# Where the high part of a split f32 weight chunk is rounded: by a cast on ScalarE, or by a transfer from GpSimd's queue

## The chip, the cores and the metric

The kernel runs on one core of a Trainium2 chip, in one launch. The metric is device time in microseconds (us), the median of repeated runs. Before the change it is 1033.94 us, the median of 3 runs that lie between 1033.83 and 1033.95.

## The reference

One decoder layer on 512 tokens of width 1024, in float32. What matters here is the long row of matrix products, each with weights of its own:

```python
h = rmsnorm(x, norm_mix_g)                        # x: 512 x 1024
proj = h @ w_in                                   # 10 sections of 512 columns, 3 x 1024 gate columns
cb, cc, ch, sq, sk, sv, rq, rk, rv, rg, gate_logits = split(proj)
branches = stack([short_conv_mixer(cb, cc, ch),   # 512 wide each
                  stick_breaking_attention(sq, sk, sv),      # 8 heads x 64
                  retention(rq, rk, rv, rg)])                # 4 heads x 128
up = einsum('bsnw,nwd->bsnd', branches, w_branch)
x = x + sum(sigmoid(gate_logits + b_gate) * up) @ w_o
h = rmsnorm(x, norm_xa_g)                         # cross-attention into 256 memory tokens, 4 heads
x = x + memory_attention(h, rmsnorm(mem), w_xq, w_xkv, w_xo)
h = rmsnorm(x, norm_mlp_g)
x = x + square(relu(h @ w_up)) @ w_down           # hidden width 4096
out = rmsnorm(x, final_g)
```

## The kernel before, in words

**Products in parts.** TensorE multiplies operands of the type fp32r, which is shorter than f32. So the kernel splits every f32 operand into a high part (the value rounded to fp32r) and a low part (what is left), and makes a product of three matmuls: high by high, high by low, low by high. This is `mm3`, lines 234 to 236. The residual stream has four token tiles of 128 rows (`x`, 128 x 1024). Each is normalised (`norm_begin`, `norm_end`: two squares with sums on ScalarE, L354; a mean on VectorE, L358; a power on GpSimd, L348, called `rstd`; a scaling on VectorE, L376, called `xn`), transposed by TensorE in eight 128 x 128 pieces (L385, into the PSUM banks called `at`), and split into `hT_h` and `hT_l` (a ScalarE cast on L223, a VectorE subtraction on L224).

**Weights as a stream.** All weights lie in DRAM as chunks of 128 x 1024 f32 (512 KB). One `Stream` holds them in the order in which the program uses them. For a chunk, SyncE's queue loads it into one of three buffers called `w_raw`; then `parts_of` takes buffers of a pool called `w_part`, 11 in number (`WBUFS`), and writes the high part (ScalarE cast, L111) and the low part (VectorE subtraction, L112). There are two kinds of chunk:

- `Plain`, 144 chunks: used as they are. One chunk feeds 24 matmuls of 512 columns, or more of fewer columns.
- `Seven`, 18 entries of two chunks: a product of a 2 x 2 block matrix made with seven block products in place of eight (L290, 256 columns each). Its weights are first combined on VectorE into `w_mix`, and then split by `parts_of` too.

**What sets the order.** The program is a list of items, `plan`; each names its chunks, and before an item runs, `pump` makes the parts of its chunks and of two more steps (`AHEAD`). The Tile framework then orders the instructions of each engine itself, from a timeline of its own, and adds the semaphores. Each engine works in its order, and a DMA queue (of SyncE, ScalarE, GpSimd) in the order in which its engine issues. When an instruction changes its engine or its cost, the order of others may change too.

**The start.** The first item issues loads of `x` tile 0, the gain `g`, two weight chunks, tile 1, a weight chunk, tiles 2 and 3. The first product is the v projection of the stick-breaking attention (`items_m` with `tok_outer`): four weight chunks, all four used for token tile 0, then for tile 1, and so on, with the normalisation of the next tile between. The accumulators of the four tiles are `mm_177`, `mm_234`, `mm_291` and `mm_348`; their normalised tiles are `xn_111`, `xn_202`, `xn_259` and `xn_316`, and the transposes of these `at_121` and `at_130`, `at_216` and `at_225`, `at_273` and `at_282`, `at_330` and `at_339`. A finished accumulator is split into `sb_v`. The four weight chunks' high parts are `w_part_143`, `w_part_149`, `w_part_155` and `w_part_161`, the low parts `w_part_144`, `w_part_150`, `w_part_156` and `w_part_162`.

**Gates and MLP.** In the later gates (`gates7`) a `Seven` entry for the gate is followed by a `Plain` chunk of `w_branch` (`w_br`). In each of the four MLP rounds `Seven` entries of `w_up` are followed by eight `Plain` chunks of `w_down`.

Of the kernel before, what the change touches and what calls it, by code (L numbers as in the profile page):

```python
# [10 lines left out]
F32 = mybir.dt.float32  # L11
F32R = mybir.dt.float32r
AF = mybir.ActivationFunctionType
ALU = mybir.AluOpType

P = 128
# [11 lines left out]
CW = 1024  # L28
# [5 lines left out]
RAWS, WBUFS, AHEAD = 3, 11, 2  # L34
# [4 lines left out]
def trunk_kernel(ctx: ExitStack, tc: tile.TileContext, x, mem, par, rot, dqd, kdec, g_mix, g_xa, g_mem, g_mlp,  # L39
                 g_fin, w_in, w_gate, w_br, w_o, w_xq, w_xk, w_xv, w_xo, w_up, w_up7, w_down, out):  # L40
    nc = tc.nc
    te, act, dve, pool = nc.tensor, nc.scalar, nc.vector, nc.gpsimd

    const = ctx.enter_context(tc.tile_pool(name="const", bufs=1))
    wpool = ctx.enter_context(tc.tile_pool(name="wpool", bufs=1))
# [18 lines left out]
    class Split:  # L64


        def __init__(self, name, n, cols=512):
            self.per = 1024 // cols
            self.n, self.cols = n, cols
            self.h = [unit(name + "_h", (P, self.per, cols)) for _ in range(n // self.per)]  # L70
            self.l = [unit(name + "_l", (P, self.per, cols)) for _ in range(n // self.per)]
# [31 lines left out]
    def parts_of(src):  # L103
        n = src.shape[1]
        part = lambda: wpool.tile([P, CW], F32R, name="w_part", bufs=WBUFS)
        if 2 * n <= CW:
            both = part()
            wh, wl = both[:, :n], both[:, n:2 * n]
        else:
            wh, wl = part(), part()  # L110
        act.copy(out=wh, in_=src)  # L111
        dve.tensor_tensor(out=wl, in0=src, in1=wh.bitcast(F32), op=ALU.subtract)  # L112
        return wh, wl

    class Plain:


        def __init__(self, t, c):
            self.loads = [(t, c)]
            self.steps = [lambda raw: parts_of(raw[0])]  # L120
            self.parts = []

        def get(self):
            return self.parts[0]
# [1026 lines left out]
```

## Time and profile before

| | |
|---|---|
| median of 3 runs | 1033.94 us (1033.83 to 1033.95) |
| the profiled execution | 1033.71 us, of which 1032.0 us are the span of the profile |
| TensorE, matmuls | busy 1015.5 us, 98% of the span, 5636 matmuls |
| VectorE | 648.8 us, 63% |
| ScalarE | 500.7 us, 49% |
| GpSimd | 66.2 us, 6% |
| read from HBM | 103.31 MB, 102 GB/s over the span with what is written |
| chain of work that ended last | TensorE 97%, DMA 1% |

A row of the timeline has the start in us, the duration, the engine (PE is TensorE, DVE is VectorE, ACT is ScalarE, POOL is GpSimd, SPq is SyncE's DMA queue), the line, the operation, the program's names for the operands, the shape and, in brackets, how long the engine was idle before and what ended that. Matmuls overlap: one starts before the last has ended, so the distance between two starts, the step, tells their rate. In the rows of groups stand the count, the busy time, the mean of one in ns, and the idle time before them with what ended most of it. In the table of windows, each engine has its busy time in the stretch with the number of instructions, in the order PE, PEld (weight loads), DVE, ACT, POOL; then come TensorE's granted clock (1.00 is full speed), the share of the DMA engines' time, and GB/s. In the list of waits stand the total, the number and the longest. In the lists of transfers, the last number is the median time from issue to landing.

### The profile page before, as it was taken

What the parts mean: (1) busy time and instruction counts of PE and PEld (TensorE: products, weight loads), DVE (VectorE), ACT (ScalarE), POOL (GpSimd) and SP (SyncE); (2) the same over time, 40 slices, a digit from 0 to 9 for tenths busy, and PEclk for the clock granted to TensorE, in tenths of its full rate; (3) what the DMA queues carried; (4) which work ended last, traced back from release to release, by engine and by line L of the source; (5) the groups of instructions that cost most, each with busy time, mean ns of one, the idle gap of its engine ahead of it and who ended that gap; (6) DMA issues with size and microseconds to landing.
All of it is one profiled execution on the core that took longest, in us unless ns stands there. A gap on an engine that the chain in (4) does not pass through costs nothing.

```text
span 1032.0 us, 14325 instructions
## 1 busy us (share of the span) xinstructions
PE 1015.5 (98%) x5636; PEld 884.9 (86%) x5636; DVE 648.8 (63%) x992; ACT 500.7 (49%) x887; POOL 66.2 (6%) x118
## 2 busy tenths in 40 slices
PE   6999999999999999999999999999999999999997
PEld 4888888888888889998898888898889989989985
DVE  5567777856563796784584555466947566565643
ACT  6465567766532154463463444345416624643741
POOL 1101112321110000000100000000000000000000
PEclk9999999999999999999999999999999999999999
DMA  6322233213122212335354213223222321332222
GB/s 265 103 102 81 83 104 102 82 42 123 62 87 79 100 62 83 103 119 198 133 184 163 82 47 118 81 83 123 86 79 82 125 92 71 124 123 80 103 85 81
DMA packets 29876, 106.33 MB, mean 103 GB/s; under 512 B 3569, under 2 KB 3569, under 8 KB 29809
## 3 DMA queue, kind: packets, MB, share of 16 engines
q1 hardware_dynamic: 27216, 98.05, 27.7%
q10 hardware_dynamic: 2592, 7.37, 2.0%
q8 instruction: 44, 0.72, 0.3%
q14 instruction: 24, 0.19, 0.1%
HBM read 103.31 MB, written 2.10 MB: 102 GB/s over the span
## 4 chain that ended last, share of the span: by engine, by line
PE 97%; DMA 1%; DVE 0%; ACT 0%; SPq 0%; issue 0%; DVEq 0%; POOLq 0%; POOL 0%
PE mm L235 24%; PE mm L234 24%; PE mm L236 24%; PE p L290 17%; PE at L385 1%; PE o L546 1%; PE aT L512 1%; DMA w_raw<-in_w_in_dram 1%; PE z L488 1%; PE z L489 0%; PE xsc L236 0%; PE xsc L235 0%; PE xsc L234 0%; PE ro L693 0%; PE sc L667 0%; PE xpp L929 0%
## 5 line engine op out<-in xcount | busy, mean ns | idle before, releaser
L112 DVE TENSOR_TENSOR w_part<-w_raw,w_part 128x1024 fp32r<-128x1024 f32 (+1 forms) x180 | 210.9, 1176 | 168.1 <-PE mm L235 75.2
L111 ACT CAST w_part<-w_raw 128x1024 fp32r<-128x1024 f32 (+1 forms) x180 | 180.6, 1006 | 135.2 <-PE mm L236 79.1
L234 PE MATMUL mm<-hT_h,w_part 128*128 128x512 f32 (+1 forms) x512 | 193.6, 379 | 0.0
L235 PE MATMUL mm<-hT_l,w_part 128*128 128x512 f32 (+1 forms) x512 | 193.3, 378 | 0.0
L236 PE MATMUL mm<-hT_h,w_part 128*128 128x512 f32 (+1 forms) x512 | 193.0, 378 | 0.0
L290 PE MATMUL p<-mix_h,w_part 128*128 128x256 f32 x576 | 112.2, 283 | 0.5 <-ACT sv_s L297 0.5
L236 PEld LDWEIGHTS mm<-hT_h,w_part 128*128 128x128 f32 x512 | 96.4, 188 | 17.1
L234 PEld LDWEIGHTS mm<-hT_h,w_part 128*128 128x128 f32 x512 | 96.2, 188 | 16.8
L235 PEld LDWEIGHTS mm<-hT_l,w_part 128*128 128x128 f32 x512 | 96.5, 188 | 16.4
L235 PE MATMUL mm<-w_part,u_h 128*128 128x512 f32 x256 | 99.8, 390 | 0.0
L234 PE MATMUL mm<-w_part,u_h 128*128 128x512 f32 x256 | 98.6, 390 | 0.0
L236 PE MATMUL mm<-w_part,u_l 128*128 128x512 f32 x256 | 98.2, 389 | 0.0
L290 PEld LDWEIGHTS p<-mix_h,w_part 128*128 128x128 f32 x576 | 93.4, 192 | 1.4 <-ACT sv_s L297 0.7
L290 PE MATMUL p<-hT_h,w_part 128*128 128x256 f32 x432 | 84.4, 283 | 0.0
L290 PE MATMUL p<-mix_l,w_part 128*128 128x256 f32 x288 | 81.5, 283 | 0.0
L290 PEld LDWEIGHTS p<-hT_h,w_part 128*128 128x128 f32 x432 | 70.1, 192 | 0.8
L111 ACT CAST w_part<-w_mix 128x1024 fp32r<-128x1024 f32 x36 | 37.8, 1051 | 55.9 <-PE mm L235 37.5
L112 DVE TENSOR_TENSOR w_part<-w_mix,w_part 128x1024 fp32r<-128x1024 f32 x36 | 44.0, 1221 | 26.7 <-ACT w_part L111 20.0
L290 PE MATMUL p<-hT_l,w_part 128*128 128x256 f32 x216 | 60.7, 283 | 0.0
L236 PEld LDWEIGHTS mm<-w_part,u_l 128*128 128x128 f32 x256 | 48.1, 188 | 9.8
L235 PEld LDWEIGHTS mm<-w_part,u_h 128*128 128x128 f32 x256 | 48.1, 188 | 9.5
L234 PEld LDWEIGHTS mm<-w_part,u_h 128*128 128x128 f32 x256 | 47.9, 188 | 9.5
(211 smaller groups left out, 1813.2 us busy)
## 6 DMA issues: line engine op xcount, KB each, us to landing
w_raw<-in_w_in_dram SPq DMA_DIRECT2D x52, 512.0 KB, 3.4
w_raw<-in_w_up_dram SPq DMA_DIRECT2D x32, 512.0 KB, 3.6
w_raw<-in_w_down_dram SPq DMA_DIRECT2D x32, 512.0 KB, 3.4
w_raw<-in_w_br_dram SPq DMA_DIRECT2D x12, 512.0 KB, 3.4
w_raw<-in_w_gate_dram SPq DMA_DIRECT2D x12, 512.0 KB, 3.5
w_raw<-in_w_o_dram SPq DMA_DIRECT2D x8, 512.0 KB, 3.5
w_raw<-in_w_xk_dram SPq DMA_DIRECT2D x8, 512.0 KB, 4.2
w_raw<-in_w_xv_dram SPq DMA_DIRECT2D x8, 512.0 KB, 3.5
```

The lines of the kernel that those rows point to most:

```text
L111: act.copy(out=wh, in_=src)
L112: dve.tensor_tensor(out=wl, in0=src, in1=wh.bitcast(F32), op=ALU.subtract)
L234: te.matmul(ps, lh, rh, start=first, stop=False)
L235: te.matmul(ps, lh, rl, start=False, stop=False)
L236: te.matmul(ps, ll, rh, start=False, stop=last)
L290: te.matmul(ps[:, :256], x[:, k, :], y, start=first and k == 0 and i == 0, stop=k == 3 and i == 2, skip_group_check=True)
L385: te.transpose(ps[:, k * P:(k + 1) * P], xn[:, c * P:(c + 1) * P], ident)
L488: te.matmul(z[:, :s], q[:, e, tsl], S["skh", hp][:, e, :s], start=True, stop=False)
L512: te.transpose(aps[:, sb * P:(sb + 1) * P], a[:, sb * P:(sb + 1) * P], ident)
L546: te.matmul(dst, vv, rhs, start=sb == 0 and i == 0, stop=sb == nblk and i == 1, skip_group_check=True)
```

## The change

A `Plain` chunk no longer goes through `parts_of`. Its high part is made by a second transfer of the same chunk from DRAM, issued from GpSimd's queue, from f32 to a tile of the type fp32r, so that the transfer rounds. SyncE still loads the chunk into `w_raw`, because VectorE's subtraction needs the f32 values. `Seven` entries keep ScalarE's cast.

```diff
         def __init__(self, t, c):
             self.loads = [(t, c)]
-            self.steps = [lambda raw: parts_of(raw[0])]
+            self.steps = [self.step]
             self.parts = []
+
+        def step(self, raw):
+            t, c = self.loads[0]
+            wh, wl = [wpool.tile([P, CW], F32R, name="w_part", bufs=WBUFS) for _ in range(2)]
+            pool.dma_start(out=wh, in_=t[c])
+            dve.tensor_tensor(out=wl, in0=raw[0], in1=wh.bitcast(F32), op=ALU.subtract)
+            return wh, wl
```

Seven lines are added, so lines behind them count 7 more: L234 to L236 become L241 to L243, L385 becomes L392, L354 becomes L361, L223 becomes L230; the new transfer is L126 and the new subtraction L127. ScalarE has 711 instructions in its order where it had 855, 144 fewer; GpSimd has 144 transfers more.

**TensorE at the start.** Before, the transposes of the second token tile (`at_216`, `at_225`) stand behind 19 matmuls of the first tile; the rows around them:

```order
L236 MATMUL mm_177<-w_part_155,hT_l_109 128x512
L234 MATMUL mm_177<-w_part_161,hT_h_106 128x512 [waits Activation_49]
L385 MATMUL at_216<-ident_73,xn_202 128x128 [waits DVE_49]
L385 MATMUL at_216<-ident_73,xn_202 128x128 x3
L385 MATMUL at_225<-ident_73,xn_202 128x128 x4
L235 MATMUL mm_177<-w_part_162,hT_h_106 128x512 [waits DVE_49]
L236 MATMUL mm_177<-w_part_161,hT_l_110 128x512
```

After, they stand behind the first six, and from there the matmuls of the first two tiles take turns; where a transferred chunk is used first, TensorE waits for GpSimd's queue (DMASW):

```order
L241 MATMUL mm_177<-w_part_143,hT_h_103 128x512
L242 MATMUL mm_177<-w_part_144,hT_h_103 128x512
L243 MATMUL mm_177<-w_part_143,hT_l_107 128x512
L392 MATMUL at_216<-ident_73,xn_202 128x128 [waits DVE_49,Activation_49]
L392 MATMUL at_216<-ident_73,xn_202 128x128 x3
L392 MATMUL at_225<-ident_73,xn_202 128x128 [waits Activation_49]
L392 MATMUL at_225<-ident_73,xn_202 128x128 x3
L241 MATMUL mm_177<-w_part_149,hT_h_104 128x512 [waits DMASW1_49]
L241 MATMUL mm_234<-w_part_143,hT_h_103 128x512 [waits Activation_49]
```

The last matmul of `mm_177` has moved next to the last ones of `mm_234`, five rows ahead of the third tile's transposes:

```order
L243 MATMUL mm_177<-w_part_161,hT_l_110 128x512
L242 MATMUL mm_234<-w_part_162,hT_h_106 128x512
L243 MATMUL mm_234<-w_part_161,hT_l_110 128x512
L241 MATMUL mm_234<-w_part_161,hT_h_106 128x512
L242 MATMUL mm_234<-w_part_162,hT_h_106 128x512
L243 MATMUL mm_234<-w_part_161,hT_l_110 128x512
L392 MATMUL at_273<-ident_73,xn_259 128x128 [waits DVE_49,PE_49,Activation_49]
```

So 48 matmuls of two tiles now end together, and the third tile's transposes stand right behind them.

**ScalarE at the start.** Before, from the first copy of a finished accumulator (`sb_v`) on:

```order
L223 CAST sb_v_139<-mm_177 128x4x64 [waits PE_49]
L223 CAST hT_h_104<-at_216 128x2x128 [waits DVE_49]
L223 CAST hT_h_106<-at_225 128x2x128 [waits DVE_49]
L223 CAST sb_v_141<-mm_177 128x4x64 [waits DVE_49]
L354 ACTIVATE xn_259,ss_260<-x_86 128x512 [waits DMAHW0_49]
L354 ACTIVATE xn_259,ss_260<-x_86 128x512
L354 ACTIVATE xn_316,ss_317<-x_87 128x512 [waits DMAHW1_49]
L354 ACTIVATE xn_316,ss_317<-x_87 128x512
L223 CAST sb_v_139<-mm_234 128x4x64 [waits PE_49]
```

After, from the same copy on:

```order
L230 CAST sb_v_139<-mm_177 128x4x64 [waits PE_49]
L230 CAST sb_v_141<-mm_177 128x4x64 [waits DVE_49]
L361 ACTIVATE xn_259,ss_260<-x_86 128x512 [waits DMAHW0_49]
L361 ACTIVATE xn_259,ss_260<-x_86 128x512
L230 CAST sb_v_139<-mm_234 128x4x64 [waits PE_49]
L361 ACTIVATE xn_316,ss_317<-x_87 128x512 [waits DMAHW1_49]
L361 ACTIVATE xn_316,ss_317<-x_87 128x512
L230 CAST sb_v_141<-mm_234 128x4x64 [waits DVE_49]
```

The squares of the third tile (`xn_259`) still stand behind the copies of `mm_177`, whose last matmul has moved; those of the fourth (`xn_316`) stand behind a copy of `mm_234` now.

**GpSimd at the start.** After, its transfers and the powers of the norms share one order; before it had the powers alone:

```order
L126 DMA w_part_143<-in_w_in_dram 128x1024
masks.py:199 ISA
masks.py:199 AFFINE_SELECT ident_73<-ident_73 128x128 [waits Pool_49]
L355 TENSOR_TENSOR rstd_118<-ms_116,half_78 128x1 [waits DVE_49,Pool_49]
L126 DMA w_part_149<-in_w_in_dram 128x1024
L355 TENSOR_TENSOR rstd_209<-ms_207,half_78 128x1 [waits DVE_49]
L126 DMA w_part_155<-in_w_in_dram 128x1024
L126 DMA w_part_161<-in_w_in_dram 128x1024
L126 DMA w_part_167<-in_w_in_dram 128x1024
L126 DMA w_part_173<-in_w_in_dram 128x1024
```

The third and later chunks' transfers stand behind the second tile's power (`rstd_209`).

**In the gates.** Before, ScalarE's cast of a `w_br` chunk stands at the place where its buffer comes free (w_part_3386 and w_part_3392 belong to the next `Seven` entry):

```order
L111 CAST w_part_3380<-w_raw_3269 128x1024 [waits DMAHW5_49,PE_49]
L744 ACTIVATE gt_3348<-mm_3323,prm_82 128x512 [waits PE_49,Activation_49]
L223 CAST mix_h_3117<-mix_3258 128x512 [waits DVE_49]
L111 CAST w_part_3386<-w_raw_3376 128x512 [waits DMAHW6_49,PE_49]
L111 CAST w_part_3392<-w_mix_3389 128x1024 [waits DVE_49,PE_49]
```

After, these are GpSimd's rows there; each transfer waits for TensorE's last use of its buffer:

```order
L355 TENSOR_TENSOR rstd_3086<-r_ve_3084,half_78 128x4 [waits DVE_49]
L126 DMA w_part_3380<-in_w_br_dram 128x1024 [waits DMASW1_49,DMASW2_49,DVE_49,PE_49]
L126 DMA w_part_3544<-in_w_br_dram 128x1024 [waits DMASW2_49,DMASW3_49,DVE_49,PE_49]
L126 DMA w_part_3708<-in_w_br_dram 128x1024 [waits DMASW3_49,DMASW4_49,DVE_49,PE_49]
L126 DMA w_part_3878<-in_w_br_dram 128x1024 [waits DMASW4_49,DMASW5_49,DVE_49,PE_49]
L126 DMA w_part_4048<-in_w_br_dram 128x1024 [waits DMASW5_49,DMASW6_49,DVE_49,PE_49]
L126 DMA w_part_4218<-in_w_br_dram 128x1024 [waits DMASW6_49,DMASW7_49,DVE_49,PE_49]
```

The step "buffer free, cast, subtraction" has become "buffer free, transfer, subtraction". On VectorE the subtraction now waits for that transfer, with work for the next entry behind it:

```order
L736 TENSOR_TENSOR gt_3348<-mm_3350,gt_3348 128x512 [waits PE_49]
L127 TENSOR_TENSOR w_part_3381<-w_raw_3269,w_part_3380 128x1024 [waits DMAHW5_49,DMASW2_49]
L144 TENSOR_TENSOR w_mix_3529<-w_raw_3378,w_mix_3529 128x512 [waits DVE_49]
L112 TENSOR_TENSOR w_part_3386<-w_raw_3376,w_part_3386 128x512 [waits Activation_49]
L737 TENSOR_TENSOR mg_2718<-mg_2718,gt_3348 128x512 [waits DVE_49]
```

Ten transferred chunks stand close to the buffer's release. Counted in TensorE's order after the change, between the matmul that frees the buffer and the first that reads the new content:

| high part | weights | matmuls between |
|---|---|---|
| `w_part_3380` | `w_br` | 14 of 512 columns, 36 of 256 |
| `w_part_3544` | `w_br` | 2 of 512, 58 of 256 |
| `w_part_3708` | `w_br` | 2 of 512, 60 of 256 |
| `w_part_3878` | `w_br` | 2 of 512, 47 of 256 |
| `w_part_4048` | `w_br` | 2 of 512, 58 of 256 |
| `w_part_4218` | `w_br` | 2 of 512, 68 of 256 |
| `w_part_4809` | `w_xk` | 19 of 512, 16 of 128, 2 of 256 |
| `w_part_7346`, `w_part_8146`, `w_part_8946` | `w_down` | 49 of 256, each |

## The prediction, made before the changed kernel ran

> **What bounds the kernel now.** I read the page's busy shares and chain first, then the span in three stretches, then who TensorE waits for, then the groups that the change touches, the transfers, and last the first 30 us in order of time.
>
> ```profile
> span 1032.0 us, 14325 instructions
> PE 1015.5 (98%) x5636; PEld 884.9 (86%) x5636; DVE 648.8 (63%) x992; ACT 500.7 (49%) x887; POOL 66.2 (6%) x118
> PE 97%; DMA 1%; DVE 0%; ACT 0%; SPq 0%; issue 0%; DVEq 0%; POOLq 0%; POOL 0%
> ...
> 0.00:30.00 30.00, 20.74 (x87) 15.91 (x88) 17.98 (x34) 18.34 (x42) 5.50 (x16) 1.00 0.60 228
> 30.00:1025.00 995.00, 994.51 (x5550) 868.97 (x5549) 628.54 (x955) 481.66 (x844) 60.18 (x101) 1.00 0.29 99
> 1025.00:1032.00 7.00, 0.21 (x1) 0.00 (x0) 2.26 (x4) 0.72 (x2) 0.55 (x1) 0.85 0.23 84
> ...
> PE at L385 <- DVE xn L376: 9.0, 2, 8.5
> PE p L290 <- ACT sv_s L297: 0.5, 1, 0.5
> ```
>
> The chain is TensorE for 97%. From 30 to 1025 us it is idle for 995.00 - 994.51 = 0.49 us, all of it in its one wait for ScalarE. So what ScalarE does there costs nothing, and there is nothing to win there. TensorE's only real idle time is 9.3 us in the first 30, and the tail. A loss, however, shows in full wherever a weight comes later than TensorE wants it.
>
> ```profile
> L112 DVE TENSOR_TENSOR w_part<-w_raw,w_part 128x1024 fp32r<-128x1024 f32 (+1 forms) x180 | 210.9, 1176 | 168.1 <-PE mm L235 75.2
> L111 ACT CAST w_part<-w_raw 128x1024 fp32r<-128x1024 f32 (+1 forms) x180 | 180.6, 1006 | 135.2 <-PE mm L236 79.1
> q1 hardware_dynamic: 27216, 98.05, 27.7%
> w_raw<-in_w_br_dram SPq DMA_DIRECT2D x12, 512.0 KB, 3.4
> w_raw<-in_w_down_dram SPq DMA_DIRECT2D x32, 512.0 KB, 3.4
> x<-in_x_dram SPq DMA_DIRECT2D x4, 512.0 KB, 8.0
> ```
>
> **The change, part by part.** Removed: 144 of the 180 casts, 144 x 1.006 = 145 us of ScalarE. Worth 0 in the 995 us stretch, whose cover is TensorE itself. The subtraction keeps its count and its 1.18 us; SyncE's loads stay. Added: 144 transfers of 512 KB, 75.5 MB. SyncE's queue used 0.277 x 1032 = 286 us of the sixteen engines for 98.05 MB, or 187 chunks: 1.53 us a chunk. Another 144 make 220 us, a share of 0.21 on top of 0.29. If the rounding transfer moves as fast as the plain one, there is room, so 0; bound above under the rivals. GpSimd's queue takes the 144 issues between its own masks and powers; in the attention part, counted in rows of TensorE's order times the steps below, the masked tile is read 8 us or more after its scores, and an issue of about 1 us (two of its 0.55 us operations, below) twice in that chain fits. A transfer there waits for a buffer that was freed long before its own use, so that a mask queued behind it on GpSimd rarely waits with it. 0, and at most a few tenths a mask if that is wrong.
>
> What costs is order and latency, at two kinds of places.
>
> **The first 30 us.** These are the rows the terms come from; in before, the second token tile's normalisation ran while TensorE worked off the first tile.
>
> ```profile
> 2.73 0.64 SPq L396 DMA_DIRECT2D x<-in_x_dram  x1
> 7.04 1.29 DVE L376 SCALAR_TENSOR_TENSOR xn<-x,rstd,g_bc 128x1024 f32<-128x1024 f32 x1 [0.74 <-POOL rstd L348]
> 8.47 1.94 PE L385 MATMUL at<-ident,xn 128*128 128x128 f32 x8 [8.47 <-DVE xn L376]
> 10.53 0.79 PE L234 MATMUL mm<-w_part,hT_h 128*128 128x512 f32 x1
> 15.01 0.63 ACT L354 ACTIVATE xn<-x 128x512 f32<-128x512 f32 x1
> 15.45 0.63 PE L235 MATMUL mm<-w_part,hT_h 128*128 128x512 f32 x1
> 15.88 0.55 PE L236 MATMUL mm<-w_part,hT_l 128*128 128x512 f32 x1
> 16.26 0.39 PE L234 MATMUL mm<-w_part,hT_h 128*128 128x512 f32 x1
> 16.49 0.40 PE L235 MATMUL mm<-w_part,hT_h 128*128 128x512 f32 x1
> 18.55 1.10 PE L385 MATMUL at<-ident,xn 128*128 128x128 f32 x8 [0.51 <-DVE xn L376]
> 21.14 0.37 ACT L223 CAST sb_v<-mm 128x256 fp32r<-128x256 f32 x1 [1.09 <-PE mm L236]
> 21.55 0.43 DVE L224 TENSOR_TENSOR sb_v<-mm,sb_v 128x256 fp32r<-128x256 f32 x1
> 22.01 0.37 ACT L223 CAST sb_v<-mm 128x256 fp32r<-128x256 f32 x1
> 22.28 0.64 ACT L354 ACTIVATE xn<-x 128x512 f32<-128x512 f32 x1
> 23.52 0.62 ACT L354 ACTIVATE xn<-x 128x512 f32<-128x512 f32 x1
> 23.65 0.16 DVE L358 SCALAR_TENSOR_TENSOR ms<-ss 128x1 f32<-128x1 f32 x1 [0.46 <-ACT xn L354]
> 23.89 0.55 POOL L348 TENSOR_TENSOR rstd<-ms,half 128x1 f32<-128x1 f32 x1 [6.72 <-DVE ms L358]
> 24.47 1.28 DVE L376 SCALAR_TENSOR_TENSOR xn<-x,rstd,g_bc 128x1024 f32<-128x1024 f32 x1
> 26.39 1.03 PE L385 MATMUL at<-ident,xn 128*128 128x128 f32 x8
> 28.02 1.04 PE L385 MATMUL at<-ident,xn 128*128 128x128 f32 x8
> ```
>
> Term 1, when the first two token tiles (48 matmuls) are done. Before, the third tile's transposes follow them at 26.39. In the changed order only 6 matmuls stand ahead of the second tile's transposes, and 42 behind. Their input starts with ScalarE's squares of the second x tile, at 15.01 before. With no casts ahead of them I put these at 13, between 12.2 (2.73, where SyncE issues that load, plus the 8.0 of its row, plus one chunk more in front) and 15.0. From the squares to the end of the normalised tile takes 24.47 + 1.28 - 22.28 = 3.47, so transposes start at 16.5. Warm, they take 1.10 and 42 matmuls at 0.227 (steps as from 16.26 to 16.49) 9.5: done at 27.1, +0.7. Slow, as the first ones are (steps of 0.43 until 16.26, 5.7 us after the first matmul), the transposes take 1.94 and half of another 5.7 us is lost: 30.8, +4.4. Which of them depends on whether 3 us of work with 2 us of idleness behind it counts towards full speed; no row says, and I take the middle, **+2.6**. GpSimd's queue has a wait in this stretch that SyncE's has not: four of the first six transfers stand behind the second tile's rstd, at 13 + 24.44 - 22.28 = 15.2. Issued there, the first lands 5 us later, at 20.2 (the price below); TensorE wants it 17 of the 42 matmuls in, at 17.6 + 3.9 = 21.5. Covered by 1.3; at 8.0 it would be 1.7 late.
>
> Term 2, the third tile. ScalarE now has its squares behind both copies of the first tile's v (mm_177), and that bank is only complete 5 matmuls before the 48 end. From that copy to the normalised tile the rows above run from 21.14 to 24.47 + 1.28 = 25.75: 4.6 us, and 0.1 to the transpose. The copy starts 0.44 after the last matmul on mm_177 starts; TensorE has 6 steps, 1.36 us, from that start. 0.44 + 4.7 - 1.36 = **3.8 us idle**, against none at 26.39 before. The fourth tile's squares follow the next copy (0.37) on ScalarE, its VectorE part follows a subtraction (0.4): its transposes start about 2.7 after the third's, where 28.02 - 26.39 = 1.6 of work is there: **1.0 us idle**. Sum 4.8, fixed by the order and hardly by any transfer.
>
> The trace shows speed falling after idleness once: the last stretch has a clock of 0.85 over 7 us, so half speed for 2.1 us, beginning 4.9 us after the last matmul. The Trainium skill ("TensorE: Matmul & The Clock Gate", Part 1) has half rate after an idle window of about 3.4 us and full rate after a busy one. By that rule a stall of 3.8 us may cost another 1.7 us (half of 3.4) behind it, and the sum would be 9.9 and not 8.2; the trace agrees in kind, at 4.9 us, and does not show 3.8.
>
> **Ten tight buffers.** Rows of TensorE's order between the last matmul on a buffer's old content and the first on its new one, times the steps, give 13 to 40 us in steady stretches. In ten places, listed with the change, they give 5.9 to 8.6 us, at 0.227 for 512 columns and 0.12 for 256, as here:
>
> ```profile
> 773.97 23.17 PE p L290 x193
> ```
>
> A cast fills such a buffer in 1.0 us. The transfer's time from the freeing matmul is not in the trace: at least SyncE's 3.4, at most the 8.0 of the crowded start. Nearest are the 3.4 rows, same size and place; GpSimd's issue (its small operations take 0.55) and the two signals make it 5 to 6. At 5 nothing is late. At 6, three down chunks miss by 0.1 each, and three first quarters of a gate's next weights, whose subtraction stands behind the transferred chunk's on VectorE, by about 0.4: 1.5 in all. I take half, **+0.8**. The Trainium skill ("DMA: Bandwidth & Descriptors", Anatomy of one DMA) gives such a transfer 2.0 us and its bytes at 436 GB/s, an estimate of 3.2 us without the issue; by it the term would be 0 and the sum 7.4.
>
> **Sum.** 2.6 + 4.8 + 0.8 = 8.2 us on the profiled execution, 1033.71 (span 1032.0 and 1.7 around it): 1041.9. The median of the runs is 0.2 above that execution: **1042**.
>
> **Rivals.** (a) Transfers are late: at 8 us the ten places miss by 0.5, 0.6, 0.35, 1.9, 0.6, 0, 1.7 and three times 2.1, in sum 12, the quarters add 1 or 2, and the first transfer behind the rstd 1.7: 1034 + 7.4 + 15 = 1056. For it: the 8.0 row and SyncE's load of the same chunk beside it. Against: in these places the queues hold one or two chunks. 0.18. (b) The rounding transfer is slower a byte, and DMA becomes the bound. A plain chunk feeds 24 x 0.227 = 5.45 us of matmuls; 1.53 of it goes to the raw load, so this decides from 3.9 us a chunk, 2.6 times the plain one. At 3 times, 0.68 us on 144 chunks: 98 us, 1130. Nothing here speaks for it. 0.06. (c) Not slower: ScalarE's relief brings the second tile's squares forward by 2 us (15.01 to 13) and term 2 vanishes, because the third tile's load or copies fall earlier than I read. 1034 - 2 = 1032, faster; it decides only if TensorE waits less than 2 us in the rows of the order, where I count 4.8. 0.07. (d) The change not doing what it says: ScalarE has exactly 144 instructions fewer in the order, so the casts are gone; if the transfer did not round, the time would be the same.
>
> **Chances.** Mine, 1037 to 1046: 0.60. The same with the start half hidden, 1036 to 1037: 0.09. (a), 1046 to 1059: 0.18. (b), above: 0.06. (c): 0.07, of which 0.04 within 0.2% (2 us, about what a measurement of this kernel tells from no change) and 0.03 faster. So slower 0.93. The range 1037 to 1059 leaves out about 0.12 below ((c) and half of the half-hidden start) and 0.06 above.
>
> **What would show it.** Right: ScalarE's busy time near 355 us, DMA share near 0.5; in the first 35 us a TensorE wait for xn of 3 to 4 us and one near 1; TensorE idle under 2 us in all from there to the tail. Wrong: no such wait (term 2), full matmul speed by 17 us (term 1 near 0.7), or TensorE waits for w_part or a DMA in the gate and down stages of more than 3 us (a), or spread over the whole span (b).

## The result, and the profile after

The changed kernel takes 1044.37 us (median of 3 runs, 1043.09 to 1045.06) against 1033.94: slower by 10.4 us. The ratio is 1.0099, 95% interval 1.0076 to 1.0122. The forecast was 1042, between 1037 and 1059. The profiled execution takes 1043.09 us, 9.4 more than that of before, where the sum had 8.2.

The page of the changed kernel, the lines that answer to those of before: span, busy time of the engines, the queues (q1 is SyncE's, q0 GpSimd's), and the chain.

```profile
span 1041.4 us, 14473 instructions
PE 1017.2 (98%) x5636; PEld 886.1 (85%) x5636; DVE 650.5 (62%) x992; ACT 362.7 (35%) x743; POOL 142.9 (14%) x262
q1 hardware_dynamic: 27216, 98.05, 26.6%
q0 software_dynamic: 20736, 75.51, 22.6%
PE 97%; DMA 1%; ACT 1%; DVE 0%; issue 0%; SPq 0%; POOL 0%; DVEq 0%; POOLq 0%
```

ScalarE has lost 138 us of work (500.7 to 362.7), and the time has grown: TensorE is the chain as before. GpSimd's 144 transfers took 0.226 x 1041.4 = 235 us of the sixteen DMA engines, 1.63 us a chunk; SyncE's plain loads 0.266 x 1041.4 = 277 us for 187, 1.48 us a chunk. So a rounding transfer costs a tenth more than a plain one, and the engines are half busy.

Where the 9.4 us went shows in one matmul, the first of the attention scores on its line (L488 before, L495 after). The two rows are from the timelines of before and of after:

```profile
55.21 0.22 PE L488 MATMUL z<-sb_kh,sb_q 128*128 128x128 f32 x1
62.69 0.22 PE L495 MATMUL z<-sb_kh,sb_q 128*128 128x128 f32 x1
```

It starts 7.48 us later; so 7.5 of the 9.4 us are lost ahead of it, and 1.9 in the 970 us that follow. The start, in the changed kernel's timeline (start, duration, and in brackets the idle time before the row and what ended it):

```profile
12.89 0.63 ACT L361 ACTIVATE xn<-x 128x512 f32<-128x512 f32 x1
15.11 1.28 DVE L383 SCALAR_TENSOR_TENSOR xn<-x,rstd,g_bc 128x1024 f32<-128x1024 f32 x1 [0.69 <-POOL rstd L355]
16.54 1.94 PE L392 MATMUL at<-ident,xn 128*128 128x128 f32 x8 [3.47 <-DVE xn L383]
28.13 0.39 PE L243 MATMUL mm<-w_part,hT_l 128*128 128x512 f32 x1
28.29 0.37 ACT L230 CAST sb_v<-mm 128x256 fp32r<-128x256 f32 x1 [0.49 <-DVE sb_v L231]
28.56 0.63 ACT L361 ACTIVATE xn<-x 128x512 f32<-128x512 f32 x1
32.19 1.21 PE L392 MATMUL at<-ident,xn 128*128 128x128 f32 x8 [3.67 <-DVE ss L375]
34.60 1.73 PE L392 MATMUL at<-ident,xn 128*128 128x128 f32 x7
```

The second tile's squares run at 12.89 and its transposes at 16.54, where TensorE has waited 3.47 us. The 48 matmuls of two tiles end with the step from 28.13, at 28.36; before, that point was 26.39, so 2.0 us are lost. Then the third tile's squares, behind the copy at 28.29, start at 28.56, and its transposes at 32.19, 3.8 us after the matmuls. The fourth tile's follow 2.41 us later, 0.8 more than before (28.02 - 26.39 = 1.63). That makes 6.6 us; the last 0.9 are lost behind it, and the clock says how. In the windows below (busy time of PE, PEld, DVE, ACT, POOL, then the granted clock), each row is one window of the grid on which the clock changes:

```profile
12.50:15.91 3.41, 0.57 (x3) 0.13 (x1) 1.54 (x4) 1.65 (x5) 1.40 (x3) 1.00 1.03 413
15.91:19.33 3.42, 2.79 (x11) 2.62 (x12) 2.45 (x5) 1.02 (x3) 1.29 (x3) 0.50 1.11 420
19.33:22.74 3.41, 3.41 (x17) 2.76 (x16) 3.04 (x5) 0.37 (x1) 0.00 (x0) 1.00 1.11 405
29.57:32.98 3.41, 0.79 (x7) 0.82 (x8) 2.33 (x6) 2.19 (x9) 0.95 (x2) 1.00 0.00 0
32.98:36.39 3.41, 3.31 (x14) 2.36 (x13) 2.96 (x6) 1.70 (x5) 0.15 (x1) 0.50 0.02 5
```

The stretches of constant clock last 3.41 us or a multiple of it. A window of this grid in which TensorE was busy only 0.57 or 0.79 us is followed by one at half speed. So each of the two waits costs twice: once itself, and once in the window behind it. Behind the third tile's wait, the slow matmuls also fill the time in which TensorE would otherwise have waited for the fourth tile, so that the list of waits below has no row for it.

Behind the start the only waits of TensorE are for a copy on ScalarE, L304 after and L297 before, now three times where it was one. From the list of TensorE's waits of after, the timeline at the second of the three, and the copy that answers to it in before:

```profile
PE at L392 <- DVE xn L383: 11.7, 2, 8.2
PE at L392 <- DVE ss L375: 3.7, 1, 3.7
PE p L297 <- ACT sv_s L304: 1.5, 3, 0.5
PE mm L242 <- DVE w_part L127: 0.3, 1, 0.3
...
890.65 0.63 ACT L1017 ACTIVATE relu<-sv 128x512 f32<-128x512 f32 x1
891.18 0.35 ACT L304 COPY sv_s<-p 128x256 f32<-128x256 f32 x1
891.59 0.39 PE L297 MATMUL p<-mix_h,w_part 128*128 128x256 f32 x1 [0.49 <-ACT sv_s L304]
879.75 0.36 ACT L297 COPY sv_s<-p 128x256 f32<-128x256 f32 x1
```

ScalarE does a relu of 512 columns ahead of the copy for which TensorE waits. In before the same copy ran at 879.75, 2.85 us ahead of the same matmul (882.60), and nothing waited. That is order again, in two MLP rounds. The 0.49 us of idle time understate what such a wait costs: the matmuls there start 0.12 us apart, and this one starts 0.77 us behind the one before it (890.82). TensorE's lag behind the kernel before is 7.86 us at the first matmul on w_down (736.81 against 728.95) and 9.31 at its last matmul (1034.13 against 1024.82), so the two added waits cost about 0.7 us each, 1.4 in all. The other 0.5 of the 1.9 us are in steps too small to name. No wait for a transferred chunk stands in the list behind the start; the row for w_part is the first chunk's, at 10.93.

### The profile page after: what moved, and what is told of

It reads as the page before. It is cut to its first block, busy times and chain, and to the rows that moved or that the text cites. A ratio compares the mean times of both kernels' runs of the same rounds, so it can differ in the third digit from the quotient of the medians.

```text
span 1041.4 us, 14473 instructions
## 1 busy us (share of the span) xinstructions
PE 1017.2 (98%) x5636; PEld 886.1 (85%) x5636; DVE 650.5 (62%) x992; ACT 362.7 (35%) x743; POOL 142.9 (14%) x262
## 4 chain that ended last, share of the span: by engine, by line
PE 97%; DMA 1%; ACT 1%; DVE 0%; issue 0%; SPq 0%; POOL 0%; DVEq 0%; POOLq 0%
PE mm L241 24%; PE mm L242 24%; PE mm L243 24%; PE p L297 17%; PE at L392 1%; PE o L553 1%; DMA x<-in_x_dram 1%; PE aT L519 1%; PE z L495 1%; PE z L496 0%; PE xsc L243 0%; PE xsc L242 0%; PE xsc L241 0%; PE ro L700 0%; PE sc L674 0%; PE xpp L936 0%
## 5 line engine op out<-in xcount | busy, mean ns | idle before, releaser
L127 DVE TENSOR_TENSOR w_part<-w_raw,w_part 128x1024 fp32r<-128x1024 f32 x144 | 176.9, 1230 | 121.2 <-PE mm L242 47.2
L241 PE MATMUL mm<-hT_h,w_part 128*128 128x512 f32 (+1 forms) x512 | 194.2, 380 | 0.0
L243 PE MATMUL mm<-hT_h,w_part 128*128 128x512 f32 (+1 forms) x512 | 193.2, 377 | 0.0
L297 PE MATMUL p<-mix_h,w_part 128*128 128x256 f32 x576 | 112.0, 283 | 1.5 <-ACT sv_s L304 1.5
L243 PEld LDWEIGHTS mm<-hT_h,w_part 128*128 128x128 f32 x512 | 96.4, 188 | 17.4
L241 PEld LDWEIGHTS mm<-hT_h,w_part 128*128 128x128 f32 x512 | 96.5, 188 | 16.5
L243 PE MATMUL mm<-w_part,u_l 128*128 128x512 f32 x256 | 99.7, 390 | 0.0
L241 PE MATMUL mm<-w_part,u_h 128*128 128x512 f32 x256 | 98.7, 389 | 0.0
L297 PEld LDWEIGHTS p<-mix_h,w_part 128*128 128x128 f32 x576 | 93.1, 191 | 2.8 <-ACT sv_s L304 2.1
L297 PE MATMUL p<-hT_h,w_part 128*128 128x256 f32 x432 | 83.7, 283 | 0.0
L297 PE MATMUL p<-mix_l,w_part 128*128 128x256 f32 x288 | 81.2, 283 | 0.0
L297 PEld LDWEIGHTS p<-hT_h,w_part 128*128 128x128 f32 x432 | 70.0, 192 | 1.0
L297 PE MATMUL p<-hT_l,w_part 128*128 128x256 f32 x216 | 60.9, 283 | 0.0
L243 PEld LDWEIGHTS mm<-w_part,u_l 128*128 128x128 f32 x256 | 48.1, 188 | 9.6
L241 PEld LDWEIGHTS mm<-w_part,u_h 128*128 128x128 f32 x256 | 47.9, 188 | 9.8
L297 PEld LDWEIGHTS p<-mix_l,w_part 128*128 128x128 f32 x288 | 55.1, 191 | 0.7
```

Source lines behind the costliest of these rows:

```text
L127: dve.tensor_tensor(out=wl, in0=raw[0], in1=wh.bitcast(F32), op=ALU.subtract)
L241: te.matmul(ps, lh, rh, start=first, stop=False)
L243: te.matmul(ps, ll, rh, start=False, stop=last)
L297: te.matmul(ps[:, :256], x[:, k, :], y, start=first and k == 0 and i == 0, stop=k == 3 and i == 2, skip_group_check=True)
```

## The experiments

All ran against the kernel before, which took 1033.7 to 1033.8 us each time.

**The first six chunks cast, the rest by transfer.**

```diff
-            self.steps = [self.step]
+            self.steps = [self.step if Plain.n >= 6 else lambda raw: parts_of(raw[0])]
+            Plain.n += 1
```

> The first six plain chunks keep ScalarE's cast, the other 138 come by transfer. ScalarE's order at the start is that of the kernel before again. Theory (the loss lies in the order of the first 47 us, 7.4 us of it in the trace, and 1.9 us more in small waits for ScalarE's copies in the MLP rounds and steps elsewhere): 1035 to 1037 us, no wait for xn over 0.5 us beside the very first, the waits of 0.5 us for sv_s still there. Rival (the 75 MB of added transfers make weights late, or tight buffers do): nearly all of the loss stays, 1042 to 1044.

Measured: 1038.32 us (1036.70 to 1040.27), ratio 1.0042 (1.0029 to 1.0055). The start is that of before to 0.1 us: the attention's first score matmul starts at 55.33. Its waits behind the start, and the timeline at the wait for x_p:

```profile
PE p L300 <- ACT sv_s L307: 1.5, 3, 0.5
PE xpp L939 <- DVE x_p L931: 0.6, 1, 0.6
...
630.55 1.23 DVE L130 TENSOR_TENSOR w_part<-w_raw,w_part 128x1024 fp32r<-128x1024 f32 x1 [2.08 <-DMA w_part<-in_w_xo_dram]
632.19 0.52 PE L939 MATMUL xpp<-ident,x_p 128*128 128x128 f32 x3 [0.60 <-DVE x_p L931]
```

So the start's loss is gone with the casts, as expected, but 4.5 us are left where 1 to 3 were expected, and its runs spread over 3.6 us, where those of before stay within 0.4. Its profiled run is one of the quicker ones (1036.98) and shows only 2.8 us in its span. The theory was incomplete. Of these 2.8 us, 1.4 are the two added waits in the MLP rounds as above, and 1.0 is lost at 632 us, where TensorE's lag grows from 0.3 to 1.3. There a transferred chunk is late: VectorE stands 2.08 us until a chunk of w_xo, issued 6.0 us earlier (624.53), has landed, and `x_p`, for which TensorE waits, stands behind that subtraction. The transfers of w_xo next to it landed in 3.7 to 4.6 us. So a late transfer can cost TensorE time without a wait for w_part in TensorE's list.

**Only the first four chunks by transfer.**

```diff
+            self.steps = [self.step if Plain.n < 4 else lambda raw: parts_of(raw[0])]
+            Plain.n += 1
```

> The opposite: only the first four plain chunks come by transfer, 140 keep the cast. Theory (order of the start): 1041 to 1043 us, with the wait of 3.7 us for the third tile's xn and two half-speed stretches of 3.4 us, as in the changed kernel, and shift of 7.4 us against the kernel before at 60 us. Rival (bytes and late weights over the whole span): 1034 to 1035.

Measured: 1042.59 us (1041.13 to 1044.44), ratio 1.0083 (1.0069 to 1.0098). Four transfers of 144, 2 of 75 MB, make 8.8 us. The rival is out: not bytes, but the order that these four casts held up. The same score matmul starts at 64.79, 9.6 us late, 2.1 more than in the changed kernel. The windows on its clock grid say why:

```profile
12.03:15.44 3.41, 0.75 (x3) 0.27 (x2) 1.63 (x5) 1.60 (x5) 1.26 (x3) 1.00 1.05 412
15.44:18.86 3.42, 2.65 (x11) 2.48 (x12) 2.45 (x4) 1.02 (x3) 0.37 (x1) 0.50 1.09 420
18.86:22.27 3.41, 3.41 (x10) 2.64 (x9) 3.19 (x5) 0.57 (x2) 0.00 (x0) 0.50 0.76 268
...
32.51:35.92 3.41, 2.58 (x10) 2.27 (x11) 2.75 (x7) 1.03 (x4) 2.03 (x4) 0.50 0.00 0
35.92:39.34 3.42, 3.42 (x13) 3.03 (x12) 2.48 (x8) 2.10 (x6) 0.59 (x2) 0.50 0.02 5
```

The grid lies 0.47 us earlier here than in the changed kernel, 2.65 and 2.58 us of work fall into the half-speed windows in place of 2.79 and 3.31, and half speed lasts two windows each time. The same order thus costs 1 to 2 us more or less by where the grid happens to lie. Whether this is also why the runs of kernels with these waits spread over 2 to 3 us is not shown: the slowest run here, 1044.44, has a mean granted clock of 0.996, and the profiled one, 1043.54, has 0.992, so the slower one spent less time at half speed.

**The normalisations ahead of the v projection, all 144 transfers kept.**

```diff
+    for t in range(1, NT):
+        item(lambda t=t: norm_x0(t))
     for t in range(NT):
         plan.append(sv[2 * t])
-        if t < NT - 1:
-            item(lambda t=t: norm_x0(t + 1))
         plan.append(sv[2 * t + 1])
```

> All 144 transfers stay; the normalisations of tiles 2 to 4 are written ahead of the v projection, so that ScalarE's squares no longer stand behind the copies of the first accumulator. Theory (second term: squares behind copies, 3.8 and 1.0 us of idle time and a half-speed stretch behind them, about 5 us in all): 1038 to 1040.5 us, without the wait of 3.7 us. Rival (the third tile's wait is one for its load, delayed by the transfers): the wait only changes its name, 1043 to 1045.

Measured: 1040.20 us (1038.89 to 1042.31), ratio 1.0065 (1.0052 to 1.0078), as the theory had it. The wait of 3.7 us is gone, and the score matmul starts at 58.56, 4.1 us ahead of the changed kernel's. The third tile did not wait for its load, but for ScalarE's squares behind the copies.

**Idle matmuls in the wait.**

```diff
+    def spin(n, of):
+        ps, w = atps("spin"), of()
+        for _ in range(n):
+            te.matmul(ps[:, :P], w, w, start=True, stop=True)
...
+        if t == 1:
+            item(lambda: spin(30, lambda: S["v"][2][:, 0, 0, :]))
```

> The changed kernel with 30 idle matmuls of 128 columns, whose result nobody reads, behind the first 48 matmuls: they run in the 3.8 us in which TensorE waits for the third tile. Nothing else in the order moves. Theory (the idle time itself costs a half-speed stretch of 3.4 us behind it, worth 1 to 1.7 us): the stretch from 33.0 to 36.4 us has full speed, and the time is 0.9 to 1.7 us below the changed kernel's. Rival (the clock falls for another reason, or what it costs is hidden by the fourth tile's wait): the same time within 0.3 us, or more by what the matmuls overrun.

Measured: 1043.23 us (4 runs, 1042.26 to 1044.13), 1.1 below the changed kernel, but the runs of the two overlap, so the time alone doesn't decide. The clock does:

```profile
15.40:18.80 3.40, 2.55 (x10) 2.44 (x11) 2.43 (x4) 0.95 (x3) 1.50 (x3) 0.50 1.09 422
18.80:22.25 3.45, 3.45 (x9) 2.65 (x8) 3.28 (x5) 0.44 (x2) 0.00 (x0) 0.50 1.12 406
28.25:31.70 3.45, 2.71 (x19) 2.16 (x17) 1.51 (x5) 2.61 (x8) 0.36 (x1) 1.00 0.03 12
31.70:35.10 3.40, 3.37 (x30) 3.13 (x30) 2.58 (x6) 1.68 (x7) 0.75 (x2) 1.00 0.02 5
```

With 2.71 us of busy time in the window of the wait, no half-speed stretch comes behind it. From the fourth tile's transposes to the score matmul nothing more is lost (a lag of 7.76, then of 7.80 us), where the changed kernel lost 0.9 (6.58, then 7.48) and the run with four transfers 1.67 (7.91, then 9.58). The first stretch, which the matmuls leave alone, took two windows in this run.

**The rest in parts.** Four runs put the cast back for all but one group of chunks, by the name of the weights. For w_down:

```diff
+            name = t.tensor.name
+            self.steps = [self.step if "w_down" in name else lambda raw: parts_of(raw[0])]
```

> Only the 32 plain chunks of w_down come by transfer; the other 112 keep the cast, the start too. With the first six chunks cast, 4.5 us of the loss were left, 2.8 of them in its trace, and its runs spread over 3.6 us. Theory (small waits that the other order makes): the two added waits of 0.5 us for sv_s, 1034.7 to 1035.2 us, and runs within 0.5 us of each other. Rival (transfers land late from time to time, at the tight buffers of w_down): 1035.5 to 1037 us, runs spread over more than 1 us, TensorE waits for w_part.

Measured: 1035.43 us (11 runs, 1035.21 to 1035.76), ratio 1.0016 (1.0008 to 1.0025). It is 1.7 us, with no spread and no wait for w_part: the two added waits for the copy (sv_s 1.5 us in three, as above) are 1.4 of it, by TensorE's lag before and behind them. Order, a little more than expected, because the expectation took only the idle time of the waits.

For w_in behind the first six chunks:

```diff
+            self.steps = [self.step if "w_in" in name and Plain.n >= 6 else lambda raw: parts_of(raw[0])]
```

> Only the plain chunks of w_in behind the first six come by transfer, 46 of them: attention, retention and the first gates, where the masks share GpSimd's queue and no buffer is tight. Theory (order): 1033.9 to 1034.4 us, runs within 0.5 us. Rival (masks or transfers are late now and then because both share GpSimd's queue): 1035 to 1037 us, runs spread over more than 1 us, TensorE waits in the attention part.

Measured: 1034.20 us (11 runs, 1034.10 to 1034.58), ratio 1.0005 (0.9996 to 1.0014). 46 transfers beside the masks on GpSimd's queue cost 0.5 us or nothing.

For all that is neither w_in nor w_down:

```diff
+            self.steps = [self.step if "w_in" not in name and "w_down" not in name else lambda raw: parts_of(raw[0])]
```

> The remaining 60 plain chunks alone by transfer: w_br, w_o, the cross-attention's weights, w_up; the cast for all others. Theory (order): the wait of 0.6 us for x_p in the cross-attention's end and 0.1 to 0.3 more, 1034.5 to 1035 us, runs within 0.5 us. Rival (late at the seven tight buffers of w_br and w_xk): 1035.5 to 1037 us, runs spread over more than 1 us, TensorE waits for w_part there.

Measured: 1036.72 us (1036.08 to 1039.35), ratio 1.0037 (1.0025 to 1.0050). The time and the spread are the rival's, 3.0 us and 3.3, but the place is not. The profiled execution (1036.61) has no wait at the buffers of w_br or w_xk. It loses 1.0 us at 635 us, where TensorE waits 0.73 us for `xv_l`, and that stands on VectorE behind the subtraction of a chunk of w_xo, which starts at 633.64, 4.7 us after its transfer was issued. Another 1.3 us are lost behind the last matmul (8.1 us to the end of the span, 6.8 before), for which no row gives a reason. So the group was split again, into w_br and the weights around the cross-attention.

```diff
+            self.steps = [self.step if "w_br" in name else lambda raw: parts_of(raw[0])]
```

> Only the 12 chunks of w_br come by transfer. Six of them are in the list of tight buffers, five still with 5.9 to 7.4 us in this order. Theory (a transfer lands 4.0 to 4.5 us after its issue, so the tight buffers are covered): 1033.6 to 1034.4 us, runs within 0.5 us, no wait of TensorE for w_part. Rival (late at the tight buffers now and then): 1035 to 1036.5 us, runs spread over more than 1 us.

Measured: 1035.14 us (11 runs, 1033.92 to 1035.52), ratio 1.0011 (1.0002 to 1.0019): 1.3 us, against the theory. The profiled run is the quickest one and has no loss, so no row shows where the others lose. What its answer on the tile w_part shows is how near it is: VectorE waits for six of the twelve chunks, and a landing takes up to 5.8 us, where the tightest buffers have 5.9 to 7.4.

```profile
  DVE w_part L128: 7.1, 6
DMA to landing us min/median/max: 3.8/4.2/5.8
```

That now and then one of them lands late enough for TensorE to wait is likely, and not shown.

```diff
+            self.steps = [self.step if any(n in name for n in ("w_o_", "w_x")) else lambda raw: parts_of(raw[0])]
```

> Only the 40 plain chunks of w_o, w_xq, w_xk, w_xv and w_xo come by transfer: the part of the program with the most bytes a us (0.6 to 0.8 of the DMA engines' time in the run with the remaining 60 chunks, landings of 5 to 6 us). Theory (the spread of up to 3.3 us and most of the 3.0 us of that run come from here, where both queues are full): 1035.5 to 1037 us, runs spread over more than 1 us. Rival (they come from w_br and w_up): 1034 to 1034.8 us, runs within 0.5 us.

Measured: 1034.98 us (11 runs, 1034.71 to 1036.84), ratio 1.0015 (1.0006 to 1.0023): 1.2 us, less than expected, with a spread of 2.1. In this part of the program the DMA engines are busier, as the windows of before and of this run show, and landings grow:

```profile
470.00:500.00 30.00, 30.00 (x145) 25.32 (x144) 16.71 (x21) 11.29 (x17) 0.56 (x1) 1.00 0.62 225
470.00:500.00 30.00, 30.00 (x139) 24.90 (x139) 12.51 (x17) 4.34 (x10) 4.15 (x7) 1.00 0.79 287
w_part<-in_w_o_dram POOLq DMA_DIRECT2D x8, 512.0 KB, 6.1
497.62 0.15 DVE L376 TENSOR_SCALAR ss<-ss 128x1 f32<-128x1 f32 x1 [3.90 <-ACT xn L362]
503.12 0.50 PE L243 MATMUL mm<-w_part,mgs 128*128 128x512 f32 x1 [0.30 <-DVE w_part L128]
```

The DMA engines are busy 0.79 of the time in place of 0.62; the transfers of w_o land 6.1 us after their issue (median), and TensorE waits for the low part of a chunk at 503 us, which costs it 0.7 us. That chunk's transfer had long landed (issued by 485.13, landed by 495.5). Its subtraction stands in VectorE's order behind the norm of a memory tile (the row at 497.62), and that tile's load, on ScalarE's queue, landed after 16.1 us, where it took 11.2 before. So what was late is a third queue's load, slowed down in the same stretch. The four groups cost 1.7 + 0.5 + 1.3 + 1.2 = 4.7 us, against 4.5 for all but the first six; the eight chunks of w_up were not tried alone.

**Each w_br chunk transferred twice.**

```diff
+            for _ in range(2):
+                pool.dma_start(out=wh, in_=t[c])
-            pool.dma_start(out=wh, in_=t[c])
```

> As the run with only w_br by transfer, but each of the 12 chunks is transferred twice, one after the other into the same buffer, so that it is there about 8.5 to 9 us after its buffer came free; in this order the buffers are free 8.9 us ahead of use. Theory (the lead counted in matmul steps is the limit; the low part, one subtraction of 1.2 us later, is what is late): six stalls of about 0.5 to 1.5 us, 1037 to 1043 us. Rival (there is slack that the count does not see): under 1035 us.

Measured: 1037.13 us (6 runs, 1036.44 to 1038.61), ratio 1.0034 (1.0022 to 1.0045), the low end of the theory. The landing of one transfer is 3.9 us (median), two make 7.8, and with issue and signals TensorE now waits for the transfer itself:

```profile
PE mm L243 <- DMA w_part<-in_w_br_dram: 1.5, 3, 0.7
  DVE w_part L129: 24.4, 12
DMA to landing us min/median/max: 3.6/3.9/5.9
```

Three stalls and not six, and VectorE waits at all twelve. The lead counted in matmul steps, 8.9 us here, is the limit to within about 1 us.

**Two runs on the start of the kernel before,** with casts only. First the normalisations ahead, as above, and idle transposes of the identity ahead of everything:

```diff
+    def warm(n):
+        ps = atps("warm")
+        for _ in range(n):
+            te.transpose(ps[:, :P], ident, ident)
+
+    item(lambda: warm(28))
```

> The kernel before, all casts, with two things that the runs at the start point to: the normalisations of tiles 2 to 4 written ahead of the v projection, and 28 transposes of the identity, whose result nobody reads, on TensorE from about 2.6 us on, so that it has full speed when the first tile comes. Theory (order and clock of the start are what TensorE's time there hangs on): full speed by 10 us in place of 16.2, and the first 40 us shorter by 0.5 to 2.5 us: 1031.5 to 1033.5 us. Rival (the start is bound by the loads, four weight chunks and four tiles at 1.3 us each): 1033.5 to 1034.5 us.

Measured: 1034.93 us (11 runs, 1034.82 to 1035.49), ratio 1.0012 (1.0004 to 1.0021): slower, against the theory. TensorE has full speed from 6.2 us on, and waits instead:

```profile
PE at L385 <- DVE ss L368: 1.7, 1, 1.7
PE mm L236 <- DVE hT_l L224: 1.2, 2, 0.6
PE mm L234 <- ACT hT_h L223: 1.1, 1, 1.1
```

What helped the changed kernel does not help the old one. Whether that is because ScalarE has casts to do among the squares was not tried apart. Then the transposes alone, with the order of before:

> The kernel before with 28 transposes of the identity ahead of the first token tile's, and no other change in the order: TensorE has full speed before the first real work. Theory (in the order of the kernel before, the first tile's matmuls wait for weights that land 1.3 us apart until 15.6 us, so that half speed until 16.2 us is hidden): 1033.4 to 1034.0 us. Rival (half speed there costs what it costs behind a stall): 1030.5 to 1032.5 us.

Measured: 1033.72 us (11 runs, 1033.62 to 1033.92), ratio 0.9999 (0.9990 to 1.0008): the same. Full speed from 5.9 us on buys nothing, since the weights land as before: the second tile's transposes start at 18.52, where they did at 18.55. Its windows on the grid:

```profile
5.90:9.31 3.41, 2.22 (x19) 1.81 (x17) 1.78 (x3) 1.22 (x3) 0.55 (x1) 1.00 1.03 416
9.31:12.73 3.42, 1.65 (x7) 0.97 (x6) 2.44 (x3) 2.18 (x4) 0.00 (x0) 1.00 1.03 422
12.73:16.14 3.41, 3.31 (x8) 1.94 (x7) 2.47 (x5) 2.00 (x8) 0.00 (x0) 0.50 1.02 407
```

No version among these beats the kernel before.

## Why the prediction was right

The time, the sign and the place were right: the loss is order at the start, and the run with four transfers and the run with six casts show it from both sides.

- **What costs nothing.** ScalarE's 138 us were indeed worth nothing, and a chunk cost 1.63 us of the DMA engines, where 1.53 had been assumed. Rival (b) is out by far, (c) too.
- **Term 1**, 2.6 within 0.7 to 4.4: 2.0. The squares start at 12.89 (13 assumed), the transposes at 16.54 (16.5). Of the two cases for the speed, the slow one came, but for one window of 3.41 us in place of the 5.7 assumed, and in other runs for two. That the middle of the two cases came near is luck.
- **Term 2**, 3.8 and 1.0: 3.8 and 0.8. It was worked out from the order and rows of before alone, and the run with the normalisations ahead confirms its cause. The sign of a TensorE wait near 1 us did not come, because half speed filled that time with slower matmuls.
- **The clock behind the wait** stood outside the sum, in the sentence on the Trainium skill. Measured: 0.9 us in the changed kernel, 1.7 in another run, 0 with the wait filled. By the rule of the Trainium skill that the prediction cites there, the sum was 9.9; that is nearer to the 9.4 of the profiled execution than the sum from the rows, 8.2, though its other terms were off too. What was wrong here is to leave out a cost because no row showed its exact case, when the tail's row showed it in kind.
- **Term 3**, 0.8 for tight buffers, is the mis-sized one. The profiled execution has no such wait. In its place stand 1.4 us for ScalarE's copies, order again, at a place of which the prediction did not speak. In the runs by group, w_br costs 1.3 us, and the weights around the cross-attention 1.2, which had been put at 0 but for one chunk of w_xk: the leads of TensorE's own reads were counted, but not that landings grow from 3.4 to over 6 us where the DMA engines are busiest, and not that other work stands on VectorE behind a subtraction that waits for its chunk: 1.0 us at w_xo in two of the profiles.
- **The number.** That 8.2 is near 9.4 is partly luck. Of the sum, 1.6 us did not come (0.6 of term 1, 0.2 of term 2, 0.8 of term 3), and 2.8 us came that were not in it (0.9 for the clock, 1.9 behind the start). The measured median lies 1.3 us above its profiled execution, where 0.2 had been assumed.
- **Not settled.** The start alone costs 8.8 us and the rest alone 4.5, together 13.3, and both at once 10.4. The two are not quite halves of the change, since the fifth and sixth chunk are cast in both. The intervals, about 1.5, 1.3 and 2.4 us to either side, allow that to be chance. Why the runs of one kernel spread by 2 to 3 us stays open: the clock grid's place may be one reason, late transfers at w_xo another; the profiles here, mostly of the quicker runs, do not tell. In which rows the slower runs with w_br lose their time no profile shows.

## What to carry to other kernels

An engine that is half idle may still be what holds an order together: taking work off it lets a scheduler put other things first, and a chain that used to run behind cover comes out in the open. Read the order after the change at the first stall that the new order could make, and work the chain out from rows of before; here that gave 4.8 us, and 4.6 were measured. A long wait of TensorE is to be priced with slower matmuls behind it: here waits of 3.5 to 3.7 us cost a further 0.9 to 1.7 us. A transfer in place of a cast is to be priced with the landing that the fullest stretch will have, not the quietest, and with all that stands behind its reader on VectorE.

## What the hardware showed that was not expected

- TensorE's clock is set window by window on a grid of 3.41 us whose place differs from run to run. At full speed, windows with 0.57, 0.75, 0.79 and 1.65 us of busy time were followed by half speed, those with 1.68 and 1.84 (the run with normalisations and idle transposes), 2.22 and 2.71 were not. So the waits need not be in one piece: in the last run, gaps of 1.2 and 0.6 us sufficed. What ends half speed is less clear. In the changed kernel and the runs with its order, windows with 2.55, 2.58 and 2.65 us kept it low, and 2.79 ended it; but in the kernel before, 3.20 us (9 matmuls, 9.37 to 12.79) left it low until 16.20, so the busy time of a window is not the whole rule. The Trainium skill ("TensorE: Matmul & The Clock Gate", Part 1) has the free-running window of 3413 ns, and the traces agree; it speaks of idle windows, where these were half to five sixths idle.
- A rounding transfer of 512 KB from GpSimd's queue costs GpSimd 0.53 us of issue, takes a tenth more of the DMA engines than a plain one, and lands 3.9 to 4.8 us after issue (medians) in the quiet parts, against 3.4 to 3.6 for SyncE's plain load before.
